# The first projections of a diffusion trunk: column sums, transposes and products in another order on TensorE, with two instead of three chunks of adaLN products on VectorE

## The chip, the cores and the metric

The kernel runs on one core of one Trainium2 chip. The metric is the device time of one execution in microseconds (us), median of several runs. Engines are named as in the profile: PE is TensorE (matmuls; PEld its weight loads), DVE is VectorE, ACT is ScalarE, POOL is GpSimd, SP is SyncE, whose queue starts nearly all DMAs. Matmuls write to PSUM; the kernel holds eight tiles (banks) of 128 x 512 floats there, six under the name `acc` and two under the name `aux`.

## The reference, cut to what matters

The whole program is two layers of a diffusion backbone over 256 latent tokens `x` and 256 context tokens `ctx`, width 1024. Only the head of layer 0 is touched:

```python
sh_m, sc_m, g_m, sh_f, sc_f, g_f = split(silu(c) @ ada_w[0] + ada_b[0], 6)   # adaLN, once for c, once for c_ctx
h = rms_norm(x, norm_mix[0]) * (1 + sc_m) + sh_m                            # and the same for ctx
y = h @ conv_w1 + b1                                                        # 1024 -> 2048
a, g = split(y, 2);  y = a * sigmoid(g)                                     # then a depthwise convolution
```

So before the first product `h @ conv_w1` can be made for a chunk of 128 features, the scale and the shift of that chunk must be there, and they are themselves products of `silu(c)` with 1 MB of `ada_w` per chunk (128 shift columns and 128 scale columns).

## The kernel before, in words

The 1024 features are eight chunks f = 0 to 7 of 128. The start of the program (L394 to L461) goes through them once and makes, for each:

- the loads (`start_load`, L363): 1 MB of adaLN weights and 256 KB of `conv_w1` for the first two output pairs, all on SP's queue;
- the adaLN sums. For most chunks (those not in `ADA_ROWS`) TensorE makes them: `ada_sums` (L239, eight matmuls of 256 columns, called S(f) below) into one PSUM bank, ACT copies the bank out (L245), two narrow matmuls sum its four partial rows into columns (`ada_cols`, L251, called C(f)), and ACT adds the bias (`ada_mods`, L258). For the chunks in `ADA_ROWS` DVE makes them instead: `start_rows` (L382), four products of 128 x 1024 with an accumulated sum, and a small bias add (L389);
- `mod_scale` on DVE (L270, writes `modA`);
- four transposes of the normed tokens into one PSUM bank (L437, called T(f)), scale and shift on ACT in that bank (L450, two halves), and the split of the result into a rounded part `ah_h` (L324, DVE) and the rest `al_h` (L325, DVE);
- the same split of the weights: `wh_w1a` on ACT (L163) and `wl_w1a` on DVE (L171);
- twelve products (L200 to L202): for two output pairs (`a0`,`g0` and `a1`,`g1`, four `acc` banks held through all eight chunks) three matmuls each, the second of which needs `al_h` and the third `wl_w1a`.

Everything of this is pinned: `pin` is `tc.keep_in_program_order`, so the order of the program text is the order on every engine's queue. An engine runs its queue in order. Before the change a chunk's round in the loop is T(f), C(f) and the modulation, then the products of chunk f-1, with S(f+1) between them; S and T both take their bank from `aux`, which has two. `ADA_ROWS` is (3, 5, 7), and `ROWS_AT` says how many of the DVE products stand ahead of the scale on ACT and how many behind the split in each round.

Ahead of that loop, `cond` is spread over the partitions by 16 matmuls (`crow`, L134) through the `aux` banks, each evicted by ACT (L136). Behind it, ACT takes the first weight block of the next pair (`wh_w1b`, L163), loads a function table, takes the sigmoid of `g0` (L467) and the biased `a0` (L479), POOL multiplies them (L480), and DVE's convolution taps (L538, L540) start on that. TensorE goes on at once with the products of the third pair (`g<-wh_w1b`).

Of the kernel before, what the change touches and what calls it, by code (L numbers as in the profile page):

```python
# [11 lines left out]
AF = mybir.ActivationFunctionType  # L12
# [3 lines left out]
P = 128  # L16
D = 1024
KC = D // P
TOK = 256
# [22 lines left out]
ADA_PAIRS += [(16 + 2 * i, 17 + 2 * i) for i in range(4)]  # L42
ADA_PAIRS += [(24 + f, 32 + f) for f in range(8)]

ADA_ROWS = (3, 5, 7)
ADA_PE = [i for i in range(20) if i not in ADA_ROWS]
ROWS_AT = [(0, 0), (0, 2), (1, 1), (1, 1), (1, 1), (1, 1), (1, 1), (0, 0)]
K_PAIRS = 2
GROUPS = [4, 4, 4, 4, 4, 4, 4, 4]
POOL = [6, 6, 6, 6, 6, 6, 6, 5]  # L50
# [31 lines left out]
def trunk_kernel(ctx: ExitStack, tc, x_in, ctx_in, cond, small, consts, rope, dist, ada, adas, adat,  # L82
                 w1a, w1b, dwd, w2, gu0, dn0, dn0l, wqk, wv, wg, wo, gu1, dn1, out):
    nc = tc.nc
# [10 lines left out]
    def acc(name):  # L95
        return ps.tile([P, 512], F32, tag="acc", name=name, bufs=6)

    def aux(name):
        return ps.tile([P, 512], F32, tag="aux", name=name, bufs=2)


    one = cp.tile([P, 1], F32, name="one")
# [9 lines left out]
    ident = cst[:, 0:128]  # L112
# [15 lines left out]

    crow0 = cv.tile([P, 4, 2 * YW], F32, tag="z4", name="crow0", bufs=Z4)
    crow0 = crow0.rearrange("p q t -> p (q t)")[:, 0:2 * D]  # L130
    for q in range(4):
        pc = aux("crow")
        for j in range(4):
            tc.keep_in_program_order(nc.tensor.matmul(pc[32 * j:32 * j + 32, :], one[0:1, :].to_broadcast([1, 32]),  # L134
                                 junk0[0:1, 512 * q:512 * q + 512], start=True, stop=True))
        nc.scalar.activation(crow0[:, 512 * q:512 * q + 512], pc, AF.Silu)  # L136

    load_tokens(x_in, 0)

# [9 lines left out]
    pin = tc.keep_in_program_order  # L149
# [6 lines left out]
    def split_hi(raw, n, name, also=lambda i: None):  # L156

        out_ = []
        for c in range(0, n, 1024):
            m = min(1024, n - c)  # L160
            hi = wp.tile([P, 1024], F32R, tag="wh", name="wh_" + name, bufs=WSPLIT)
            lo = wp.tile([P, 1024], F32R, tag="wl", name="wl_" + name, bufs=WSPLIT)
            also(nc.scalar.activation(hi[:, :m], raw[:, c:c + m], AF.Copy))  # L163
            out_.append((hi, lo))
        return out_

    def split_lo(raw, n, parts, eng=None, also=lambda i: None):
# [190 lines left out]
    h = new_act(pA, "h0")  # L358
# [3 lines left out]
    w1r, w1br, ada0 = {}, {}, {}  # L362

    def start_load(i):
        if i in ADA_ROWS:
            ada0[i] = [sp.tile([P, D], F32, tag="k4", name=f"raw_ada{i}", bufs=K4) for _ in range(2)]
            for c in range(2):
                pin(nc.sync.dma_start(ada0[i][c], adas[ADA_ROWS.index(i), :, D * c:D * c + D]))
        else:
# [22 lines left out]
    xs = normed([0, 1], xn4[:, 0:2, :]) + normed([2, 3], xn4[:, 2:4, :])  # L392
# [2 lines left out]
    dw = smc("dw").rearrange("p (c t) -> p c t", c=KC)  # L395
    dwb = smc("dwb")
    cn = smc("cn")
    pa0 = [(acc(f"a{p}"), acc(f"g{p}")) for p in range(K_PAIRS)]
    w1a_w = {}

    def start_products(f, p):
        wh, wl = w1a_w[f]
        for g in range(2):
            c = slice(256 * p + 128 * g, 256 * p + 128 * g + 128)
            mm3(pa0[p][g], (wh[:, c], wl[:, c]), (h[0][:, f, :], h[1][:, f, :]), f == 0, f == KC - 1, pin)

    def start_sums(f):
        if f < KC and f not in ADA_ROWS:
            pa = ada_sums(f, ada0.pop(f), aux, pin)
            ada_mid0[f] = pa, ada_rows(f, pa, pin)  # L410

    def start_w(f):
        if f < KC:
            w1a_w[f] = split_hi(w1r[f], 256 * K_PAIRS, f"w1a{f}", pin)[0]
            split_lo(w1r[f], 256 * K_PAIRS, [w1a_w[f]], None, pin)

    ada_mid0 = {}
    for n in range(3):
        start_load(n)
    start_sums(0)  # L420
    gens = {f: start_rows(f) for f in ADA_ROWS}
    rows = [f for f in ADA_ROWS for _ in range(4)]

    def piece(n):
        for _ in range(min(n, len(rows))):
            next(gens[rows.pop(0)])

    for f in range(KC + 1):
        if f + 3 < KC:
            start_load(f + 3)  # L430
        elif f + 3 == KC:
            w1_load(K_PAIRS)
            w1_load(K_PAIRS + 1)
        if f < KC:
            pt = aux("tr_start")
            for i in range(4):
                pin(nc.tensor.transpose(pt[:, P * i:P * i + P], xs[i][:, P * f:P * f + P], ident))  # L437
            if f == 1:
                start_products(0, 0)
            if f not in ADA_ROWS:  # L440
                ada_cols(f, *ada_mid0[f], pin)
                ada_mods(f, ada_mid0[f][0], pin)
            else:
                for _ in gens[f]:
                    pass
            pin(mod_scale(0, 0, f, f + 1))
            piece(ROWS_AT[f][0])
            for s in range(2):
                A, B = mod_AB(0, 0, f, s)
                pin(nc.scalar.activation(pt[:, TOK * s:TOK * s + TOK], pt[:, TOK * s:TOK * s + TOK], AF.Identity,  # L450
                                         scale=A, bias=B))
            if f == 0:
                start_w(0)
            split_to(h[0][:, f, :], h[1][:, f, :], pt, pin)
            piece(ROWS_AT[f][1])
        if f > 1:
            start_products(f - 1, 0)
        start_sums(f + 1)
        start_w(f + 1)
        if f:  # L460
            start_products(f - 1, 1)  # L461

    yc = cv.tile([P, KC, 512], F32, tag="big", name="yc")

# [168 lines left out]
    for step in range(KC):  # L633
        d = step - 1
        c = max(step - 2, 0) if step > 1 else None
        if d >= 0:
            pool_taps(d)
        if step < K_PAIRS:
            pa, pg = pa0[step]
            sg = sgs[step] or glu_gate(step, pg)  # L640
        else:
            if step == 3:
                pg, pa = acc(f"g{step}"), acc(f"a{step}")
            else:
                pa, pg = acc(f"a{step}"), acc(f"g{step}")
# [44 lines left out]
        if step >= KC - 3:  # L690
            i = 2 * (step - KC + 3)
# [8 lines left out]
    c, d = KC - 2, KC - 1  # L700
# [89 lines left out]
    nh, pt = ptk[:, 8:12], ptk[:, 12:16]  # L790
# [45 lines left out]
    crow = ad.tile([P, 2, D], F32, name="crow")  # L836
# [26 lines left out]
    for n in range(2):  # L863
# [7 lines left out]
        for t, k in order:  # L871
# [11 lines left out]
            if n and (t, k) == (1, KC - 1):  # L883
                mod_scale(0, 1)
                h = new_act(pB, "h0f")
# [24 lines left out]
    for gi, (j0, gn) in enumerate(groups):  # L910
        hid = new_act(pA, f"hid{gi}")
        for j in range(j0, j0 + gn):
# [3 lines left out]
            pa, pb = acc(f"fa{j}"), acc(f"fb{j}")  # L916
# [33 lines left out]
        else:  # L950
            for n in range(2):
# [4 lines left out]
                for t, k in order:  # L956
# [5 lines left out]
                    if n and (t, k) == (1, gn - 1):  # L962
# [3 lines left out]
                        h = new_act(pB, "h1")  # L966
# [100 lines left out]
    for hd in range(HEADS):  # L1067
# [41 lines left out]
        for which in range(2):  # L1109
            pt = aux(f"qkT{hd}{which}").rearrange("p (d t) -> p d t", d=2)  # L1110
# [94 lines left out]
        else:  # L1205
# [11 lines left out]
            h = new_act(pB, "h1f")  # L1217
# [233 lines left out]
```

## Time and profile before

| | us |
|---|---|
| median of 3 runs | 1101.7 (1098.86 to 1102.46) |
| the profiled execution | 1103.33 |
| its span in the trace | 1101.2 |
| PE busy in the span | 1069.0 (97%) |
| DVE, ACT, POOL busy | 700.6, 417.5, 161.6 |

The profiled execution's own time is 2.1 us more than its span, and 1.6 us over the median of the runs. The share of busy PE is high over the whole span, so a table by stretches is needed to see what bounds the first 60 us. [...]

### The profile page before, as it was taken

What the parts mean: (1) busy time and instruction counts of PE and PEld (TensorE: products, weight loads), DVE (VectorE), ACT (ScalarE), POOL (GpSimd) and SP (SyncE); (2) the same over time, 40 slices, a digit from 0 to 9 for tenths busy, and PEclk for the clock granted to TensorE, in tenths of its full rate; (3) what the DMA queues carried; (4) which work ended last, traced back from release to release, by engine and by line L of the source; (5) the groups of instructions that cost most, each with busy time, mean ns of one, the idle gap of its engine ahead of it and who ended that gap; (6) DMA issues with size and microseconds to landing.
All of it is one profiled execution on the core that took longest, in us unless ns stands there. A gap on an engine that the chain in (4) does not pass through costs nothing.

```text
span 1101.2 us, 13492 instructions
## 1 busy us (share of the span) xinstructions
PE 1069.0 (97%) x5302; PEld 845.0 (77%) x5302; DVE 700.6 (64%) x1147; ACT 417.5 (38%) x607; POOL 161.6 (15%) x119
## 2 busy tenths in 40 slices
PE   6989998999999999999999999999999989999998
PEld 2766654789888888888888788888888868888886
DVE  3988873757999877545644796366364555555445
ACT  4474463343222122212232564234333454444442
POOL 0077853030000000000000330000000461000000
PEclk8999998999999999999999999999999999999999
DMA  9469778732566576533313342334333344455551
GB/s 372 181 179 264 223 195 348 265 115 99 191 248 249 201 296 234 186 114 116 115 59 132 135 143 106 115 134 155 113 115 115 115 152 155 172 190 191 190 182 49
DMA packets 35185, 190.29 MB, mean 173 GB/s; under 512 B 3953, under 2 KB 4401, under 8 KB 16177
## 3 DMA queue, kind: packets, MB, share of 16 engines
q1 hardware_dynamic: 34688, 187.87, 49.0%
q10 hardware_dynamic: 434, 1.55, 0.4%
q8 instruction: 42, 0.69, 0.3%
q14 instruction: 21, 0.17, 0.0%
HBM read 185.99 MB, written 3.42 MB: 172 GB/s over the span
## 4 chain that ended last, share of the span: by engine, by line
PE 86%; DVE 6%; DMA 4%; ACT 3%; issue 1%; SPq 0%; POOL 0%; ACTq 0%; DVEq 0%
PE u L202 4%; PE fa L201 4%; PE u L200 4%; PE u L201 4%; PE fa L202 4%; PE fb L201 4%; PE fb L202 4%; PE fa L200 4%; PE fb L200 4%; PE v L201 3%; PE v L202 3%; PE v L200 3%; PE dn L201 3%; PE dn L202 3%; PE dn L200 3%; PE cv L507 2%
## 5 line engine op out<-in xcount | busy, mean ns | idle before, releaser
L171 DVE TENSOR_TENSOR wl_gu<-raw_gu,wh_gu 128x1024 fp32r<-128x1024 f32 x76 | 92.2, 1223 | 82.6 <-ACT wh_gu L163 81.7
L163 ACT ACTIVATE wh_gu<-raw_gu 128x1024 fp32r<-128x1024 f32 x84 | 88.0, 1058 | 139.6 <-PE fb L201 52.6
L851 DVE SCALAR_TENSOR_TENSOR junk<-raw_adat,crow 128x1024 f32<-128x1024 f32 x80 | 97.5, 1219 | 0.9
L171 DVE TENSOR_TENSOR wl_dn<-raw_dn,wh_dn 128x1024 fp32r<-128x1024 f32 x38 | 46.5, 1224 | 45.3 <-ACT wh_dn L163 45.0
L200 PE MATMUL fa<-ah_h0f,wh_gu 128*128 128x512 f32 (+1 forms) x192 | 72.0, 376 | 1.0 <-DVE ah_h0f L324 1.0
L201 PE MATMUL fa<-al_h0f,wh_gu 128*128 128x512 f32 (+1 forms) x192 | 72.3, 376 | 0.1
L200 PE MATMUL fb<-ah_h0f,wh_gu 128*128 128x512 f32 (+1 forms) x192 | 72.1, 376 | 0.0
L202 PE MATMUL fa<-ah_h0f,wl_gu 128*128 128x512 f32 (+1 forms) x192 | 72.0, 375 | 0.0
L202 PE MATMUL fb<-ah_h0f,wl_gu 128*128 128x512 f32 (+1 forms) x192 | 72.0, 375 | 0.0
L201 PE MATMUL fb<-al_h0f,wh_gu 128*128 128x512 f32 (+1 forms) x192 | 72.0, 375 | 0.0
L163 ACT ACTIVATE wh_dn<-raw_dn 128x1024 fp32r<-128x1024 f32 x38 | 40.3, 1060 | 80.1 <-PE dn L202 35.5
L200 PE MATMUL u<-wh_gu,ah_h1f 128*128 128x512 f32 x160 | 63.5, 397 | 0.0
L171 POOL TENSOR_TENSOR wl_qk<-raw_qk,wh_qk 128x1024 fp32r<-128x1024 f32 x4 | 9.6, 2401 | 362.8 <-DVE res L355 350.3
L202 PE MATMUL u<-wh_gu,al_h1f 128*128 128x512 f32 x160 | 62.8, 393 | 0.0
L201 PE MATMUL u<-wl_gu,ah_h1f 128*128 128x512 f32 x160 | 62.2, 390 | 0.0
L523 POOL TENSOR_TENSOR pacc<-pacc,pr 128x512 f32<-128x512 f32 x39 | 58.8, 1508 | 17.8 <-ACT pr L522 15.5
L540 DVE SCALAR_TENSOR_TENSOR lacc<-y,sm,lacc 128x512 f32<-128x512 f32 x65 | 49.1, 755 | 2.1
L201 PE MATMUL v<-wl_v,ah_h 128*128 128x512 f32 x128 | 50.4, 393 | 0.0
L202 PE MATMUL v<-wh_v,al_h 128*128 128x512 f32 x128 | 50.1, 391 | 0.0
L200 PE MATMUL dn<-wh_dn,ah_hid 128*128 128x512 f32 x128 | 49.9, 390 | 0.0
L201 PE MATMUL dn<-wl_dn,ah_hid 128*128 128x512 f32 x128 | 49.8, 389 | 0.0
L202 PE MATMUL dn<-wh_dn,al_hid 128*128 128x512 f32 x128 | 49.8, 389 | 0.0
(308 smaller groups left out, 2669.5 us busy)
## 6 DMA issues: line engine op xcount, KB each, us to landing
raw_gu<-in_gu_dram SPq DMA_DIRECT2D x44, 1024.0 KB, 4.8
raw_adat<-in_adat_dram SPq DMA_DIRECT2D x28, 1024.0 KB, 4.9
raw_dn<-in_dn_dram SPq DMA_DIRECT2D x19, 1024.0 KB, 4.8
raw_ada<-in_ada_dram SPq DMA_DIRECT2D x10, 1024.0 KB, 10.8
z<-yd SPq DMA_DIRECT2D x32, 284.5 KB, 4.9
raw_qk<-in_wqk_dram SPq DMA_DIRECT2D x8, 1024.0 KB, 4.7
raw_v<-in_wv_dram SPq DMA_DIRECT2D x8, 1024.0 KB, 4.8
raw_g<-in_wg_dram SPq DMA_DIRECT2D x8, 1024.0 KB, 4.8
```

The lines of the kernel that those rows point to most:

```text
L163: also(nc.scalar.activation(hi[:, :m], raw[:, c:c + m], AF.Copy))
L171: also((eng or nc.vector).tensor_tensor(lo[:, :m], raw[:, c:c + m], hi[:, :m].bitcast(F32), op=ALU.subtract))
L200: also(nc.tensor.matmul(o, a[0], b[0], start=first, stop=False))
L201: also(nc.tensor.matmul(o, a[0], b[1], start=False, stop=False))
L202: also(nc.tensor.matmul(o, a[1], b[0], start=False, stop=last))
L507: pin(nc.tensor.matmul(cb[32 * q:32 * q + 32, :], dg[:, g, q, :], m, start=(g == 0), stop=(g == n - 1)))
L523: pin(nc.gpsimd.tensor_tensor(pacc, pacc, pr, op=ALU.add))
L540: pin(nc.vector.scalar_tensor_tensor(cacc, a, w, cacc, op0=ALU.mult, op1=ALU.add))
L851: pin(nc.vector.scalar_tensor_tensor(junk, raw[:, c, :], 1.0, crow[:, s, :], op0=ALU.mult, op1=ALU.mult, accum_out=mods[l][:, c0 + c, s:s ...
```

## The change

Four things change, all in the first 60 us.

1. The `crow` matmuls write four `acc` banks, not two `aux` banks in turn; ACT's evictions move in the text, and the banks `a0`, `g0`, `a1`, `g1` are taken afterwards.
2. S(f) takes its bank from `acc` (two are left there), so `aux` holds nothing but transposes.
3. The loop is written as a pipeline: in round f stand T(f+1), then the first three products of chunk f, then C(f+1) and the whole modulation of chunk f+1 (ACT and DVE), then the other nine products of chunk f, then S(f+2). The weight split of a chunk stands behind the split of its tokens.
4. `ADA_ROWS` is (4, 6), not (3, 5, 7), so TensorE makes the sums of one chunk more and DVE four products less; `ROWS_AT` puts the DVE products into rounds 2 to 5, between the rounds' tokens.

```diff
-ADA_ROWS = (3, 5, 7)
+ADA_ROWS = (4, 6)
-ROWS_AT = [(0, 0), (0, 2), (1, 1), (1, 1), (1, 1), (1, 1), (1, 1), (0, 0)]
+ROWS_AT = [(0, 0), (0, 0), (0, 3), (1, 0), (0, 3), (1, 0), (0, 0), (0, 0)]
...
+    pcs = [acc(f"crow{q}") for q in range(4)]
     for q in range(4):
-        pc = aux("crow")
...
-            pa = ada_sums(f, ada0.pop(f), aux, pin)
+            pa = ada_sums(f, ada0.pop(f), acc, pin)
...
-        if f < KC:
-            pt = aux("tr_start")
-            for i in range(4):
-                pin(nc.tensor.transpose(pt[:, P * i:P * i + P], xs[i][:, P * f:P * f + P], ident))
-            if f == 1:
-                start_products(0, 0)
-            if f not in ADA_ROWS:
-                ada_cols(f, *ada_mid0[f], pin)
-                ada_mods(f, ada_mid0[f][0], pin)
-            else:
-                for _ in gens[f]:
-                    pass
-            pin(mod_scale(0, 0, f, f + 1))
-            piece(ROWS_AT[f][0])
...
-            split_to(h[0][:, f, :], h[1][:, f, :], pt, pin)
-            piece(ROWS_AT[f][1])
-        if f > 1:
-            start_products(f - 1, 0)
-        start_sums(f + 1)
-        start_w(f + 1)
-        if f:
-            start_products(f - 1, 1)
+        piece(ROWS_AT[f][0])
+        more = f + 1 < KC
+        if more:
+            start_T(f + 1)
+        start_products(f, 0, 0)
+        if more:
+            start_cols(f + 1)
+            start_h(f + 1)
+        start_products(f, 0, 1)
+        start_products(f, 1, 0)
+        start_products(f, 1, 1)
+        start_sums(f + 2)
+        piece(ROWS_AT[f][1])
```

`start_T`, `start_cols` and `start_h` are the old loop's lines as functions; `start_h` ends with the weight split `start_w(f)`.

On DVE, from the low part of chunk 3's weights (`wl_w1a_316` before, `wl_w1a_344` now) to the tokens of the row chunk behind it. Before, `raw_ada_287` and `raw_ada_288` are the row weights of chunk 5:

```order
L171 TENSOR_TENSOR wl_w1a_316<-raw_w1a_205,wh_w1a_315 128x512
L389 TENSOR_TENSOR mods_111<-mods_111,sm 128x2x2
L270 SCALAR_TENSOR_TENSOR modA_113<-mods_111,sm 128x2
L382 SCALAR_TENSOR_TENSOR junk_77,mods_111<-raw_ada_287,crow_84 128x1024
L324 CAST ah_h_121<-tr_start 128x512
L325 TENSOR_TENSOR al_h_122<-tr_start,ah_h_121 128x512
L382 SCALAR_TENSOR_TENSOR junk_77,mods_111<-raw_ada_287,crow_84 128x1024
L171 TENSOR_TENSOR wl_w1a_360<-raw_w1a_242,wh_w1a_359 128x512
```

Now, `raw_ada_275` and `raw_ada_276` are the row weights of chunk 4, and `wl_w1a_381` is chunk 4's:

```order
L170 TENSOR_TENSOR wl_w1a_344<-raw_w1a_232,wh_w1a_343 128x512
L381 SCALAR_TENSOR_TENSOR junk_77,mods_107<-raw_ada_275,crow_84 128x1024 x2
L381 SCALAR_TENSOR_TENSOR junk_77,mods_107<-raw_ada_276,crow_84 128x1024 x2
L388 TENSOR_TENSOR mods_107<-mods_107,sm 128x2x2
L269 SCALAR_TENSOR_TENSOR modA_109<-mods_107,sm 128x2
L323 CAST ah_h_117<-tr_start 128x512
L324 TENSOR_TENSOR al_h_118<-tr_start,ah_h_117 128x512
L170 TENSOR_TENSOR wl_w1a_381<-raw_w1a_279,wh_w1a_380 128x512
```

The products that stood singly, ahead of a cast and behind a split, now stand four in a row between the weights of chunk 3 and the scale of chunk 4; the same stands between chunks 5 and 6.

On PE, where a chunk with sums on TensorE follows. Before, `ada_348` is chunk 4's sum bank and `w1a_315` are the weights of chunk 3:

```order
L437 MATMUL tr_start<-cst,xn_125 128x128 x4
L251 MATMUL ada_348<-cst,adasb 128x2 x2
L200 MATMUL a_174<-ah_h_121,wh_w1a_315 128x512
L201 MATMUL a_174<-al_h_122,wh_w1a_315 128x512
L202 MATMUL a_174<-ah_h_121,wl_w1a_316 128x512
L200 MATMUL g_175<-ah_h_121,wh_w1a_315 128x512
```

Now, `ada_393` is chunk 5's sum bank and `w1a_380` are the weights of chunk 4:

```order
L238 MATMUL ada_393<-raw_ada_322,csil 32x256 x8
L418 MATMUL tr_start<-cst,xn_121 128x128 x4
L199 MATMUL a_226<-ah_h_117,wh_w1a_380 128x512
L200 MATMUL a_226<-al_h_118,wh_w1a_380 128x512
L201 MATMUL a_226<-ah_h_117,wl_w1a_381 128x512
L250 MATMUL ada_393<-cst,adasb 128x2 x2
L199 MATMUL g_227<-ah_h_117,wh_w1a_380 128x512
```

The column sums of a chunk stood ahead of all products of the chunk before it; now they stand behind the first three of them.

## Rows read from the trace of the kernel before

**Rows 1.** The table by stretches, busy time of each engine in two stretches of 10 us, with granted clock and DMA.

```profile
core 0: us, PE busy (x) PEld busy (x) DVE busy (x) ACT busy (x) POOL busy (x), PEclk, DMA share, GB/s
20.00:30.00 10.00, 8.83 (x38) 6.34 (x39) 4.43 (x8) 2.39 (x6) 0.00 (x0) 0.52 1.04 414
...
40.00:50.00 10.00, 9.24 (x58) 6.74 (x56) 9.77 (x20) 4.58 (x12) 0.00 (x0) 1.00 0.09 34
```

**Rows 2.** The chain of waits that ended last, in order of time: start, length, what. A load of row weights, a pair of DVE products, and the end of the stage.

```profile
9.95 12.01 DMA raw_ada<-in_adas_dram
...
47.71 1.22 DVE junk L382 x2
...
55.42 1.92 ACT wh_w1b L163 x2
...
60.00 1.20 POOL y L480
```

**Rows 3.** Instructions in order of time (start, length, engine, line, what; in brackets the idle time before it and what ended it): chunk 0 and the way of chunk 1 from its column sums to its split.

```profile
12.53 1.93 PE L239 MATMUL ada<-raw_ada,csil 128*32 128x256 f32 x16 [0.56 <-DMA raw_ada<-in_ada_dram]
...
14.39 1.12 PE L437 MATMUL tr_start<-cst,xn 128*128 128x128 f32 x4
...
14.52 0.39 ACT L245 ACTIVATE adasb<-ada 128x256 f32<-128x256 f32 x1 [1.89 <-PE ada L239]
...
15.30 0.84 PE L251 MATMUL ada<-cst,adasb 128*128 128x2 f32 x4
...
16.64 1.07 PE L239 MATMUL ada<-raw_ada,csil 128*32 128x256 f32 x16 [0.50 <-ACT mods L258]
...
20.67 1.08 PE L437 MATMUL tr_start<-cst,xn 128*128 128x128 f32 x4 [2.96 <-DVE al_h L325]
...
24.11 0.85 PE L251 MATMUL ada<-cst,adasb 128*128 128x2 f32 x4
25.00 0.41 ACT L258 ACTIVATE mods<-ada,sm 128x2 f32<-128x2 f32 x2 [5.73 <-PE ada L251]
...
25.64 1.11 ACT L450 ACTIVATE tr_start<-tr_start,mods,modA 128x256 f32<-128x256 f32 x2 [0.23 <-DVE modA L270]
...
26.78 0.69 DVE L324 CAST ah_h<-tr_start 128x512 fp32r<-128x512 f32 x1 [1.18 <-ACT tr_start L450]
...
27.51 0.69 DVE L325 TENSOR_TENSOR al_h<-tr_start,ah_h 128x512 fp32r<-128x512 f32 x1
...
28.11 1.21 DVE L382 SCALAR_TENSOR_TENSOR junk<-raw_ada,crow 128x1024 f32<-128x1024 f32 x1
...
30.52 0.69 DVE L171 TENSOR_TENSOR wl_w1a<-raw_w1a,wh_w1a 128x512 fp32r<-128x512 f32 x1
```

**Rows 4.** The same view later: a weight split, the bias of a row chunk and its scale on ACT; the splits of chunks 3 and 7; the first product of the third pair on PE.

```profile
35.11 0.69 DVE L171 TENSOR_TENSOR wl_w1a<-raw_w1a,wh_w1a 128x512 fp32r<-128x512 f32 x1
...
35.71 0.15 DVE L389 TENSOR_TENSOR mods<-mods,sm 128x4 f32<-128x4 f32 x1
...
36.16 1.11 ACT L450 ACTIVATE tr_start<-tr_start,mods,modA 128x256 f32<-128x256 f32 x2 [3.01 <-DVE modA L270]
...
38.03 0.69 DVE L325 TENSOR_TENSOR al_h<-tr_start,ah_h 128x512 fp32r<-128x512 f32 x1
...
56.18 0.69 DVE L325 TENSOR_TENSOR al_h<-tr_start,ah_h 128x512 fp32r<-128x512 f32 x1
...
59.55 0.39 PE L200 MATMUL g<-ah_h,wh_w1b 128*128 128x512 f32 x1
```

**Rows 5.** The same view, PE alone, for its pace: two products at the lower clock, then column sums and transposes with what follows each, and ten products in a row at the higher clock.

```profile
21.98 0.63 PE L201 MATMUL a<-al_h,wh_w1a 128*128 128x512 f32 x1
...
22.41 0.63 PE L202 MATMUL a<-ah_h,wl_w1a 128*128 128x512 f32 x1
...
30.31 0.51 PE L251 MATMUL ada<-cst,adasb 128*128 128x2 f32 x4
...
30.68 0.48 PE L200 MATMUL a<-ah_h,wh_w1a 128*128 128x512 f32 x1
...
33.53 0.60 PE L437 MATMUL tr_start<-cst,xn 128*128 128x128 f32 x4
...
33.88 0.47 PE L200 MATMUL a<-ah_h,wh_w1a 128*128 128x512 f32 x1
...
40.24 0.39 PE L202 MATMUL a<-ah_h,wl_w1a 128*128 128x512 f32 x1
...
42.28 0.39 PE L202 MATMUL g<-ah_h,wl_w1a 128*128 128x512 f32 x1
```

**Rows 6.** PE in short stretches late in the program (busy time, granted clock, DMA): an idle gap and the clock behind it.

```profile
904.00:905.00 1.00, 0.00 (x0) 1.00 0.97 410
...
908.00:909.00 1.00, 1.00 (x4) 0.50 0.97 401
...
911.00:912.00 1.00, 1.00 (x6) 1.00 0.83 303
```

**Rows 7.** Instructions of PE that waited, 69 to 92 us.

```profile
71.94 3.64 PE L507 MATMUL cv<-z,dg 128*32 128x512 f32 x32 [1.35 <-issue]
...
82.58 3.64 PE L507 MATMUL cv<-z,dg 128*32 128x512 f32 x32 [1.32 <-ACT pr L522]
```

More of the change, by code (lines that the diff above doesn't have):

```diff
@@ L130, in trunk_kernel @@
     crow0 = crow0.rearrange("p q t -> p (q t)")[:, 0:2 * D]
+    pcs = [acc(f"crow{q}") for q in range(4)]
     for q in range(4):
-        pc = aux("crow")
         for j in range(4):
-            tc.keep_in_program_order(nc.tensor.matmul(pc[32 * j:32 * j + 32, :], one[0:1, :].to_broadcast([1, 32]),
+            tc.keep_in_program_order(nc.tensor.matmul(pcs[q][32 * j:32 * j + 32, :], one[0:1, :].to_broadcast([1, 32]),
                                  junk0[0:1, 512 * q:512 * q + 512], start=True, stop=True))
-        nc.scalar.activation(crow0[:, 512 * q:512 * q + 512], pc, AF.Silu)
     load_tokens(x_in, 0)
@@ L397, in trunk_kernel, with start_products, start_T, start_cols @@
     cn = smc("cn")
-    pa0 = [(acc(f"a{p}"), acc(f"g{p}")) for p in range(K_PAIRS)]
     w1a_w = {}
[L401 to L405, printed above, removed]
+    def start_products(f, p, g):
+        wh, wl = w1a_w.get(f)
+        c = slice(256 * p + 128 * g, 256 * p + 128 * g + 128)
+        mm3(pa0[p][g], (wh[:, c], wl[:, c]), (h[0][:, f, :], h[1][:, f, :]), f == 0, f == KC - 1, pin)
+    ada_mid0, tr0 = {}, {}
     def start_sums(f):
         if f < KC and f not in ADA_ROWS:
-            pa = ada_sums(f, ada0.pop(f), aux, pin)
+            pa = ada_sums(f, ada0.pop(f), acc, pin)
             ada_mid0[f] = pa, ada_rows(f, pa, pin)
     def start_w(f):
-        if f < KC:
-            w1a_w[f] = split_hi(w1r[f], 256 * K_PAIRS, f"w1a{f}", pin)[0]
-            split_lo(w1r[f], 256 * K_PAIRS, [w1a_w[f]], None, pin)
-    ada_mid0 = {}
+        w1a_w[f] = split_hi(w1r[f], 256 * K_PAIRS, f"w1a{f}", pin)[0]
+        split_lo(w1r[f], 256 * K_PAIRS, [w1a_w[f]], None, pin)
+    def start_T(f):
+        tr0[f] = aux("tr_start")
+        for i in range(4):
+            pin(nc.tensor.transpose(tr0[f][:, P * i:P * i + P], xs[i][:, P * f:P * f + P], ident))
+    def start_cols(f):
+        if f not in ADA_ROWS:
+            ada_cols(f, *ada_mid0[f], pin)
+            ada_mods(f, ada_mid0[f][0], pin)
+        else:
+            for _ in gens[f]:
+                pass
+    def start_h(f):
+        pt = tr0.pop(f)
+        pin(mod_scale(0, 0, f, f + 1))
+        for s in range(2):
+            A, B = mod_AB(0, 0, f, s)
+            pin(nc.scalar.activation(pt[:, TOK * s:TOK * s + TOK], pt[:, TOK * s:TOK * s + TOK], AF.Identity,
+                                     scale=A, bias=B))
+        split_to(h[0][:, f, :], h[1][:, f, :], pt, pin)
+        start_w(f)
     for n in range(3):
@@ L426, in piece @@
             next(gens[rows.pop(0)])
-    for f in range(KC + 1):
+    start_cols(0)
+    start_T(0)
+    start_h(0)
+    for q in range(4):
+        nc.scalar.activation(crow0[:, 512 * q:512 * q + 512], pcs[q], AF.Silu)
+    start_sums(1)
+    pa0 = [(acc(f"a{p}"), acc(f"g{p}")) for p in range(K_PAIRS)]
+    for f in range(KC):
         if f + 3 < KC:
@@ L433, in trunk_kernel @@
             w1_load(K_PAIRS + 1)
-        if f < KC:
-            pt = aux("tr_start")
-            for i in range(4):
-                pin(nc.tensor.transpose(pt[:, P * i:P * i + P], xs[i][:, P * f:P * f + P], ident))
-            if f == 1:
-                start_products(0, 0)
-            if f not in ADA_ROWS:
-                ada_cols(f, *ada_mid0[f], pin)
-                ada_mods(f, ada_mid0[f][0], pin)
-            else:
-                for _ in gens[f]:
-                    pass
-            pin(mod_scale(0, 0, f, f + 1))
-            piece(ROWS_AT[f][0])
[L448 to L453, printed above, removed]
-            split_to(h[0][:, f, :], h[1][:, f, :], pt, pin)
-            piece(ROWS_AT[f][1])
-        if f > 1:
-            start_products(f - 1, 0)
-        start_sums(f + 1)
-        start_w(f + 1)
-        if f:
-            start_products(f - 1, 1)
+        piece(ROWS_AT[f][0])
[11 more added lines that the diff above has]
+        piece(ROWS_AT[f][1])
     yc = cv.tile([P, KC, 512], F32, tag="big", name="yc")
```

## The prediction, made before the changed kernel ran

> **What bounds the kernel now.** I read the table by stretches first, since a share of 97% for PE over the whole span says nothing of one stage. [...] Then the chain of waits, in order of time: up to 22 us it hangs on the load of chunk 3's row weights, afterwards on DVE (pairs of products, splits) with a scale on ACT in each round, and after 55.42 us on ACT and POOL, up to the first convolution input `y` at 60.00 us [rows 2]. The instructions in order of time say what the early stretch waits for: T(1) starts at 20.67 us after 2.96 us of idle PE, because its bank in `aux` is chunk 0's until `al_h` has been written [rows 3]. Chunk 3's split starts at 38.03 us and chunk 7's at 56.18, so two chunks take 9.08 us there [rows 4].
>
> So the stage has two halves: up to chunk 2 waits and a slow clock, then DVE. The sums below give c(f), the time at which the column sums of chunk f end on PE; all else of a chunk hangs on it.
>
> **The change, part by part.** *From column sums to split.* In the rows of chunk 1, C ends at 24.96, the scale starts on ACT at 25.64 (0.68 later), the cast at 26.78, `al_h` at 27.51 (2.55 after c), and the next DVE instruction at 28.11, 3.15 after c [rows 3]. Now that next one is the weight split of 0.69, so it ends 3.84 after c. Behind it PE has the third product of the chunk (0.23: ten products lie 0.227 apart, 40.24 to 42.28) and C of the next chunk (0.37: 30.31 to 30.68) [rows 5]. With 0.05 for the handover, as between C's end and ACT's start (24.96 to 25.00) [rows 3], a chunk takes 3.84 + 0.05 + 0.23 + 0.37 = 4.5 us. PE's own work is 12 x 0.227 + 0.35 (T) [rows 5] + 1.07 (S) [rows 3] + 0.37 = 4.5, so at the higher clock both just match.
>
> *The first chunks.* S(0) waits for its load at 12.53 us as before, and ACT's copy ends at 14.91 [rows 3]. C(0) now stands ahead of T(0): 14.96 + 0.84 = 15.80, T(0) then takes 1.12 and ends at 16.92, and the scale waits for T(0) where it waited for C(0): start at 16.96, as if c(0) were 16.3. Before it was 16.14, so this swap gains nothing. Then c(1) = 20.8 against 24.96, c(2) = 25.3, c(3) = 29.8. T(1) and S(1) need no bank of chunk 0 any more, and that is where the gain comes from. Chunk 3's `al_h` starts at 29.8 + 2.55 = 32.35 against 38.03 [rows 4]: 5.7 us gained.
>
> *The two row chunks.* Four DVE products stand in one piece behind `wl_w1a` of chunk 3, ahead of the scale of chunk 4, and again between 5 and 6. Nothing on DVE can pass them, and C(5) on PE stands behind the products of chunk 4, which need chunk 4's split. Step by step from c(3): `wl_w1a` starts at +3.15, the next instruction 0.60 later (35.11 to 35.71) [rows 4]; two products take 2.41 (28.11 to 30.52) [rows 3], four 4.82, to +8.57; from the bias to the scale on ACT 0.45 (35.71 to 36.16) [rows 4], +9.02; cast 1.14 later, `al_h` 0.73 after that (26.78 to 27.51) [rows 3], `wl_w1a` 0.60 after that, ended at +12.18; handover, product and C(5) 0.65: c(5) = c(3) + 12.8 = 42.6, and c(7) = 55.4. Two chunks took 9.08 before, so 3.7 are lost in each of two rounds, 7.4 in all, against a gain of 5.7. Three row chunks of DVE work have become two, but the products that lay beside ACT's scale (DVE was never idle there) now lie with nothing beside them, and DVE is idle for the scale.
>
> *The end of the stage.* ACT ends chunk 7's scale 1.8 after c(7), at 57.2, then has this chunk's weight split (0.6, estimated: DVE's takes 0.69 on the same tile, ACT's `wh_w1b` blocks of twice the width 0.96 each [rows 2]) that stood earlier before, so it comes to `wh_w1b` at 57.8 against 55.42 [rows 2]. What follows on ACT is unchanged, so `y` comes 2.4 us later. PE's way: 24 products of chunks 6 and 7 at 0.227 and the wait for `wl_w1a` (59.2) give 59.2 + 0.05 + 12 x 0.227 = 62.0 against 59.55 [rows 4], also 2.4.
>
> *The clock.* PE now idles in each row round: it ends T(5) at c(3) + 2.04 + 0.35, waits for `wl_w1a` (33.64), then 0.28 + 2.04 + 1.07 + 0.35 = 37.4, and chunk 4's cast ends at 40.65, a gap of 3.3 us, twice. Before, the gap of 2.96 us ahead of T(1) was followed by the stretch at 0.52 [rows 1, 3], and a gap around 904 us by some 3 us at 0.50 [rows 6]. So I take the lower level behind both gaps. There a product takes 0.43 (21.98 to 22.41) [rows 5] and C 0.85 [rows 3], so the last step before c(5) and c(7) is longer by 0.20 + 0.48 = 0.68 each: 1.4 in all. Bounds: nothing (the gaps are forgiven) and 2.6, if the twelve products of chunk 7 run at that level too (12 x 0.20 on PE, of which the 1.35 us of idle PE before the first convolution [rows 7] hide half).
>
> *The rest.* The `crow` matmuls lose two waits on ACT but S(0) waits for its load anyway. S of one chunk more (1.07) lies in PE's row-round idle time. The row weights: chunk 3's landed at 21.96 [rows 2]; a chunk's 1.25 MB at 414 GB/s [rows 1] is 3.2 us, so chunk 4's are there at about 25 (estimate), 8 us ahead of need. SP's queue: S(0) must free a raw buffer before chunk 3's load can be issued, at 14.5 instead of 9.6, while the loads of chunks 1 and 2 still fill the DMA; cost nothing, and if the DMA ran dry meanwhile, at most the 4.9 us of delay less the 5 that chunk 3's S has in hand (its data at 22, its turn at 25.3 + 2.04 = 27.3): nothing again.
>
> Sum: 2.4 + 1.4 = 3.8 us, own range 2.4 to 5. Behind the stage the DVE taps start from `y`, so I pass it on whole. The profiled execution would go from 1103.3 to 1107.1; it stood 1.6 over the median of the runs, so against that median: 1101.7 + 3.8 = 1105.5.
>
> **The rivals.** *The slow clock stays in the first half too.* For it: PE between 17 and 20 us has only sums, transposes and three single products, and it fell to 0.50 there before. Against: there is no gap of 3 us left. One spell as long as that of 904 us costs half of its 3.3 us, 1.6; the stretch up to 29.6, at 12 x 0.43 + 1.93 + 0.91 (T to C, 14.39 to 15.30) + 0.85 = 8.8 us per chunk [rows 3, 5], costs 0.7 for chunk 1 and 4.3 for chunk 2. 1107 to 1110.5, about 1108.5. [...]
>
> *The convolution stage swallows it: not slower.* PE idles 1.35 and 1.32 us before the first two convolution groups [rows 7]. If those waits are for something that does not move with `y`, PE takes 2.7 of the 3.8 us back, from 71.94 us on: 1101.7 + 1.1 = 1102.8, or 1101.4 with the clock kept. Against: what is waited for there comes out of `y` by the bounce through memory and ACT's taps.
>
> *The row products cost nothing: faster.* If DVE reached chunk 5 as fast as before, the 5.7 us would stay: 1101.7 - 5.7 = 1096. For it: DVE has four products of 1.21 us less to do [rows 3]. Against: the order on its queue, and C(5) behind chunk 4's products. It wins if the step from the split of chunk 3 to that of chunk 5 stays below 11.9 us (9.08 + half of 5.7).
>
> **How the numbers follow.** The forecast has 50%, the slow first half 22%, the swallowed delay 16%, the kept gain 10%, anything else 2%. About 0.3% (3.3 us) is what a measurement can tell from no change: of the forecast's range 2.4 to 5, some 36 of the 50 lie above it. Slower: 0.36 + 0.21 = 0.57; same: 0.14 + 0.16 + 0.02 = 0.32; faster 0.11. The range goes from 1101 (the swallowed delay) to 1109.5 (most of the slow first half), and leaves out the kept gain and the rest of the slow clock.
>
> **What would show it.** Right: `al_h` of chunks 1, 2 and 3 near 23.4, 27.9 and 32.4 us; four row products without a break on DVE at about 33.5; a gap of some 3 us on PE that ends with a product that waited for the cast; `al_h` of chunk 7 near 58 to 59; `y` on POOL at 62 to 64. Wrong: chunk 3's split later than 35 us (then the clock or a load), chunk 5's less than 11.9 us after chunk 3's (then the row round is not what I take it for), or `y` later by 3 us and the end not.

## The result and the profile after

The changed kernel takes 1105.85 us (median of 11 runs, 1102.0 to 1108.55) beside 1100.88 us (11 runs, 1098.04 to 1102.8) for the kernel before: ratio 1.0041 [1.0026, 1.0055], slower by 4.5 us (1100.88 x 0.0041) to 5.0 (the medians). The profiled execution took 1106.84 us, its span 1105.0 against 1101.2. The busy times over the whole span show nothing of the loss: PE is busy for 1072.4 us, 97% as before.

The table by stretches shows the stage, and answers to [rows 1] (PEclk is the granted clock of TensorE as a share of its full one):

```profile
core 0: us, PE busy (x) PEld busy (x) DVE busy (x) ACT busy (x) POOL busy (x), PEclk, DMA share, GB/s
20.00:30.00 10.00, 10.00 (x72) 7.24 (x72) 4.26 (x8) 4.83 (x12) 0.00 (x0) 1.00 1.02 405
30.00:40.00 10.00, 8.73 (x52) 5.83 (x51) 7.16 (x14) 2.04 (x5) 0.00 (x0) 1.00 0.76 289
40.00:50.00 10.00, 7.75 (x24) 5.97 (x25) 5.48 (x11) 3.92 (x9) 0.00 (x0) 0.66 0.24 100
50.00:60.00 10.00, 7.15 (x42) 4.70 (x41) 6.11 (x12) 3.35 (x9) 0.00 (x0) 0.94 0.00 1
```

From 20 to 30 us PE is now full, and at the higher clock from about 21 us on (the durations tell this, C(1) 0.77 us at 20.62 and C(2) 0.50 at 25.68, not the column PEclk, which reads 1.00 also from 16 to 18 us, where S(1) takes 1.94 us). From 40 us on nothing is full: DVE, which was busy for 9.77 of 10 us there, is busy for 5.48 and PE for 7.75 at a granted clock of 0.66. A stage in which each engine waits for another has taken the place of one that DVE bounded.

The instructions in order of time (start, length; the idle time before it in brackets), which answer to [rows 3] and [rows 4]. First the pipeline's pace, then the row round of chunk 4, then the end of the stage:

```profile
20.62 0.77 PE L250 MATMUL ada<-cst,adasb 128*128 128x2 f32 x4
...
25.68 0.50 PE L250 MATMUL ada<-cst,adasb 128*128 128x2 f32 x4
...
30.51 0.50 PE L250 MATMUL ada<-cst,adasb 128*128 128x2 f32 x4
...
33.55 0.69 DVE L324 TENSOR_TENSOR al_h<-tr_start,ah_h 128x512 fp32r<-128x512 f32 x1
...
34.76 1.22 DVE L381 SCALAR_TENSOR_TENSOR junk<-raw_ada,crow 128x1024 f32<-128x1024 f32 x1
...
38.55 1.22 DVE L381 SCALAR_TENSOR_TENSOR junk<-raw_ada,crow 128x1024 f32<-128x1024 f32 x1
...
39.82 0.17 DVE L388 TENSOR_TENSOR mods<-mods,sm 128x4 f32<-128x4 f32 x1
...
42.25 0.76 PE L199 MATMUL a<-ah_h,wh_w1a 128*128 128x512 f32 x1 [3.20 <-ACT adasb L244]
...
44.08 0.85 PE L250 MATMUL ada<-cst,adasb 128*128 128x2 f32 x4
...
45.41 0.16 DVE L269 SCALAR_TENSOR_TENSOR modA<-mods,sm 128x2 f32<-128x2 f32 x1 [1.98 <-ACT mods L257]
...
47.48 0.69 DVE L324 TENSOR_TENSOR al_h<-tr_start,ah_h 128x512 fp32r<-128x512 f32 x1
...
57.75 0.50 PE L250 MATMUL ada<-cst,adasb 128*128 128x2 f32 x4
...
60.79 0.69 DVE L324 TENSOR_TENSOR al_h<-tr_start,ah_h 128x512 fp32r<-128x512 f32 x1
...
65.13 1.19 POOL L493 TENSOR_TENSOR y<-y,sg 128x512 f32<-128x512 f32 x1 [63.76 <-ACT y L492]
...
77.00 3.64 PE L520 MATMUL cv<-z,dg 128*32 128x512 f32 x32 [1.39 <-issue]
```

And chunk 5's split in the kernel before:

```profile
47.10 0.69 DVE L325 TENSOR_TENSOR al_h<-tr_start,ah_h 128x512 fp32r<-128x512 f32 x1
```

Chunk 3's split starts 4.5 us earlier than before (33.55 against 38.03 [rows 4]). Then four products of DVE stand in a row, 34.76 to the bias add at 39.82, while PE idles for 3.20 us and comes back at about half the pace: the granted clock is 0.50 from 42 to 48 us, and the column sums at 44.08 take 0.85, not 0.50. DVE waits in turn: `modA` of chunk 5 comes after 1.98 us of idle DVE, because PE made C(5) only behind chunk 4's first three products. Chunk 5's split is 0.4 us late (47.48 against 47.10), chunk 7's is 4.6 us late (60.79 against 56.18), `y` 5.1 (65.13 against 60.00 [rows 2]), the first convolution group 5.1 (77.00 against 71.94 [rows 7]).

PE alone in a full round of the pipeline, behind the column sums at 25.68, which answers to [rows 5]; between 26.37 and 27.99 stand six more products:

```profile
26.04 0.49 PE L199 MATMUL g<-ah_h,wh_w1a 128*128 128x512 f32 x1
26.37 0.40 PE L200 MATMUL g<-al_h,wh_w1a 128*128 128x512 f32 x1
...
27.99 0.40 PE L201 MATMUL g<-ah_h,wl_w1a 128*128 128x512 f32 x1
28.32 1.07 PE L238 MATMUL ada<-raw_ada,csil 128*32 128x256 f32 x16
29.32 0.66 PE L418 MATMUL tr_start<-cst,xn 128*128 128x128 f32 x4
29.73 0.48 PE L199 MATMUL a<-ah_h,wh_w1a 128*128 128x512 f32 x1
30.05 0.39 PE L200 MATMUL a<-al_h,wh_w1a 128*128 128x512 f32 x1
```

The next instruction begins before the one ahead of it has ended, so the pace is read from start to start: 0.36 us behind the column sums, then nine products up to 28.32, the sums 1.00, the transposes 0.41, three products to 30.51.

The chain of waits (start, length, what) hangs in the row round on the products, then on ACT, PE and ACT again, where before it went from DVE to ACT's scale and back in each round [rows 2]:

```profile
38.55 1.24 DVE junk L381 x2
...
42.25 0.76 PE a L199
...
44.28 0.66 PE ada L250 x4
...
60.58 1.89 ACT wh_w1b L162 x2
```

### The profile page after: what moved, and what is told of

Same layout as the page of the kernel before. It is cut to its first block, busy times and chain, and to the rows that moved or that the text cites. A ratio compares the mean times of both kernels' runs of the same rounds, so it can differ in the third digit from the quotient of the medians.

```text
span 1105.0 us, 13526 instructions
## 1 busy us (share of the span) xinstructions
PE 1072.4 (97%) x5322; PEld 847.0 (77%) x5322; DVE 696.3 (63%) x1138; ACT 418.2 (38%) x610; POOL 161.6 (15%) x119
## 4 chain that ended last, share of the span: by engine, by line
PE 85%; DVE 4%; DMA 4%; ACT 3%; POOL 2%; issue 2%; SPq 0%; ACTq 0%; POOLq 0%
PE fa L200 4%; PE fa L201 4%; PE fb L201 4%; PE fa L199 4%; PE fb L200 4%; PE fb L199 4%; PE u L201 3%; PE u L199 3%; PE u L200 3%; PE v L200 3%; PE v L201 3%; PE v L199 3%; PE dn L199 3%; PE dn L200 3%; PE dn L201 3%; PE g L199 2%
```

## The experiments

Eleven runs were made, eight of other kernels and three of the two kernels as they are. Ratios are against the kernel before, timed on the same chip with each set (1101.52 us for the first four, 1101.19 for the next four; 1101.31 in a single run beside the last three). `y` is the start of its product on POOL: 60.00 before, 65.13 after. The first part of the change, the banks of `crow`, was not run alone; S(0), which stands behind it, starts at 12.33 to 12.53 us in three traces of the kernel before and at 12.23 and 12.48 in two of the changed one, so no effect of it can be seen.

**1. One product less in each block.**

```diff
-ROWS_AT = [(0, 0), (0, 0), (0, 3), (1, 0), (0, 3), (1, 0), (0, 0), (0, 0)]
+ROWS_AT = [(0, 0), (0, 1), (0, 3), (0, 1), (0, 3), (0, 0), (0, 0), (0, 0)]
```

> The changed kernel with one of each row chunk's four DVE products moved one round ahead, behind the weight split of the chunk before, where DVE waits for the next scale. Theory (the DVE products that stand in one piece are the loss): each product taken out of a block brings its 1.26 us, the moved one lies in idle time; y on POOL from 65.1 to about 62.7 us, time about 2.4 us below the changed kernel's, 1103.4. Rival (the loss is PE's: a pace of 4.8 us per chunk and the clock behind the gaps): no change, y at 65.

Measured: 1103.24 us, ratio 1.0016 [1.0005, 1.0027], `y` at 62.53, as the theory has it. Each product that stands beside another wait takes 1.3 us off a round (2.6 in two). The gaps of PE shrink to 1.93 and 0.97 us; the first is still followed by the lower clock (0.50 from 42 to 47 us), the second not (1.00 from 50 to 60):

```profile
40.92 0.63 PE L199 MATMUL a<-ah_h,wh_w1a 128*128 128x512 f32 x1 [1.93 <-ACT adasb L244]
...
53.57 0.47 PE L199 MATMUL a<-ah_h,wh_w1a 128*128 128x512 f32 x1 [0.97 <-ACT adasb L244]
```

**2. The same eight products, each where DVE waits anyway:** one behind `modA`, while ACT scales, and one at the end of a round.

```diff
-ROWS_AT = [(0, 0), (0, 0), (0, 3), (1, 0), (0, 3), (1, 0), (0, 0), (0, 0)]
+ROWS_AT = [(0, 0), (0, 1), (0, 1), (0, 1), (0, 1), (0, 0), (0, 0), (0, 0)]
+ROWS_IN = [0, 0, 1, 1, 1, 1, 0, 0]
...
         pin(mod_scale(0, 0, f, f + 1))
+        piece(ROWS_IN[f])
```

> The changed kernel with the eight DVE products spread singly: one behind modA (beside ACT's scale) and one behind the weight split in chunks 2 to 5. Theory: the row rounds go at PE's pace of 4.8 us per chunk like the others, chunk 7's column sums end at about 50.5 instead of 58.3, no gap of 3 us on PE and no fall of the clock there; y at about 57.5, time about 1098, below the kernel before. Rival: PE's pace and the first half bound it, y above 62 and time above 1103.

Measured: 1098.02 us, ratio 0.9970 [0.9958, 0.9982], `y` at 56.64: 8.5 us earlier than in the changed kernel, with the same work. In the order of time a product fills the time between `modA` and the cast, and no gap of PE over 0.5 us is left between 20 and 58 us:

```profile
31.20 0.16 DVE L270 SCALAR_TENSOR_TENSOR modA<-mods,sm 128x2 f32<-128x2 f32 x1 [0.32 <-ACT mods L258]
31.28 1.22 DVE L382 SCALAR_TENSOR_TENSOR junk<-raw_ada,crow 128x1024 f32<-128x1024 f32 x1
32.43 0.08 DVE L382 DVE_READ_ACCUMULATOR junk<-raw_ada,crow 128x1 f32 x1
32.54 0.69 DVE L324 CAST ah_h<-tr_start 128x512 fp32r<-128x512 f32 x1
```

**3. No row products:** `ADA_ROWS = ()`, so TensorE makes the sums of all eight chunks; nothing is left out.

> The changed kernel with all eight chunks' sums on TensorE and no DVE products (ADA_ROWS empty). It takes S(4), C(4), S(6), C(6) more on PE, 2 x 1.4 us. Theory: all rounds take 4.8 us, chunk 7's column sums end at 21.4 + 6 x 4.8 = 50.2, y at about 57, time about 1097.5. Rival (TensorE's sums are the dearer ones, or the raw buffers' loads come late): y at 60 or later, time 1101 or more.

Measured: 1097.52 us, ratio 0.9966 [0.9954, 0.9978], `y` at 56.81. The column sums start every 4.8 us (30.18, 34.96, 39.79, 44.61, 49.42) with PE full: the pipeline runs at PE's pace throughout, and ends no earlier than with the eight products well placed.

**4. The kernel before with the sums' bank alone,** in the old order and with the old rows:

```diff
-            pa = ada_sums(f, ada0.pop(f), aux, pin)
+            pa = ada_sums(f, ada0.pop(f), acc, pin)
```

> The kernel before with one edit: S(f) takes its bank from acc, so T(1) does not wait for chunk 0's split. Theory (the early gain comes from the banks, not from the pipeline's order): T(1) at about 18 instead of 20.7, chunk 1's column sums end at about 22 instead of 25, chunk 3's al_h 2 to 3 us earlier than 38.0; then DVE's pace of 9.1 us for two chunks as before, so y at 57 to 58 and time about 1098.5. Rival (the early gain needs the pipeline's order): y at 59.5 to 60, time as before.

Measured: 1097.27 us, ratio 0.9961 [0.9947, 0.9975], `y` at 56.69. This one line gains 4.3 us (2.8 to 5.8 by the interval), though the loads, which the chain of waits names for the first 22 us [rows 2], are as they were. T(1) no longer waits for chunk 0's `al_h` (16.59 against 20.67 [rows 3]), PE stays at the higher pace behind it (C(1) takes 0.50 us, where it took 0.85 [rows 3]), and the 3.3 us that chunk 3 is ahead (34.72 against 38.03) stay to the end of the stage. PE idles for 2.21 and 1.60 us on the way, and the granted clock stays at 1.00 behind both (the products behind them take 0.39 to 0.40 us):

```profile
16.59 0.66 PE L437 MATMUL tr_start<-cst,xn 128*128 128x128 f32 x4
...
19.46 0.47 PE L200 MATMUL a<-ah_h,wh_w1a 128*128 128x512 f32 x1 [2.21 <-DVE ah_h L324]
...
21.33 0.50 PE L251 MATMUL ada<-cst,adasb 128*128 128x2 f32 x4
...
30.07 0.50 PE L200 MATMUL a<-ah_h,wh_w1a 128*128 128x512 f32 x1 [1.60 <-DVE ah_h L324]
...
34.72 0.69 DVE L325 TENSOR_TENSOR al_h<-tr_start,ah_h 128x512 fp32r<-128x512 f32 x1
...
52.87 0.69 DVE L325 TENSOR_TENSOR al_h<-tr_start,ah_h 128x512 fp32r<-128x512 f32 x1
```

**5. The changed kernel with its gaps of PE filled** by twelve extra products whose result is not used:

```diff
             start_T(f + 1)
+        if f in ADA_ROWS:
+            pf = acc("fill")
+            for _ in range(12):
+                pin(nc.tensor.matmul(pf, w1a_w[f - 1][0][:, 0:128], h[0][:, f - 1, :], start=True, stop=True))
```

> The changed kernel with twelve products more on TensorE in each of the two gaps (2.7 us, into a free bank, their result unused), ahead of the first product of chunks 4 and 6. Theory (the half-rate spells cost about 0.9 us at chunk 5 and up to 1 at the end): the clock stays at 1.00 from 41 to 64 us, chunk 5's column sums end near 44.0 instead of 44.9, y at about 64, time 1 to 2 us below the changed kernel's, 1104 to 1105. Rival (the clock costs nothing, since DVE is waited for): y at 65, time 1106.

Measured: 1103.15 us, ratio 1.0016 [1.0007, 1.0025], `y` at 64.12. The granted clock is 1.00 behind both gaps and up to `y`, and the order's own price is left over:

```profile
20.47 0.50 PE L250 MATMUL ada<-cst,adasb 128*128 128x2 f32 x4
...
33.14 0.69 DVE L324 TENSOR_TENSOR al_h<-tr_start,ah_h 128x512 fp32r<-128x512 f32 x1
...
38.40 3.02 PE L469 MATMUL fill<-ah_h,wh_w1a 128*128 128x512 f32 x12
...
41.84 0.47 PE L199 MATMUL a<-ah_h,wh_w1a 128*128 128x512 f32 x1 [0.43 <-ACT adasb L244]
...
46.46 0.69 DVE L324 TENSOR_TENSOR al_h<-tr_start,ah_h 128x512 fp32r<-128x512 f32 x1
...
59.77 0.69 DVE L324 TENSOR_TENSOR al_h<-tr_start,ah_h 128x512 fp32r<-128x512 f32 x1
```

The step from chunk 3's split to chunk 5's is 13.32 us, where the changed kernel takes 13.93: the slow clock costs 0.61 in the first round. From chunk 5 to chunk 7 it is 13.31 in both, so nothing in the second. The other 0.4 us in `y` were there before the first gap (33.14 against 33.55): PE came up earlier in this execution, C(1) took 0.50 us and not 0.77, and chunk 1's split starts at 23.51 against 23.94. The median fell by 2.7, more than `y`, but each ratio is uncertain by 0.1% to 0.15%, and what the run has beyond 0.6 to 1.0 us is not explained.

**6. C(5) and C(7) ahead of the row chunk's products:**

```diff
             start_T(f + 1)
+        if f in ADA_ROWS:
+            start_cols(f + 1)
         start_products(f, 0, 0)
         if more:
-            start_cols(f + 1)
+            if f not in ADA_ROWS:
+                start_cols(f + 1)
```

> The changed kernel with the column sums C(5) and C(7) ahead of the first three products of chunks 4 and 6 on TensorE, nothing else moved. Theory (DVE waits for C(5) behind those products, 45.41 less 43.43 = 2.0 us): DVE goes from chunk 4's weight split to chunk 5's modA at once, 1.3 to 2.0 us per row round; y at 61.5 to 62.5, time about 1102.5 to 1103. Rival (the four DVE products are all of the loss): y at 64.5 to 65, time 1105 to 1106.

Measured: 1102.53 us, ratio 1.0010 [1.0000, 1.0020], `y` at 62.12, 3 us earlier than in the changed kernel, as the theory has it. C(5) now starts with chunk 4's split and no longer behind three products that need it. What it still waits for is ACT's copy of its bank (L244), which stands on ACT behind chunk 4's scale and weight split, so the four DVE products ahead of that scale still hold it up:

```profile
41.94 0.37 ACT L244 ACTIVATE adasb<-ada 128x256 f32<-128x256 f32 x1
...
42.36 1.01 PE L250 MATMUL ada<-cst,adasb 128*128 128x2 f32 x4 [3.18 <-ACT adasb L244]
...
54.62 0.61 PE L250 MATMUL ada<-cst,adasb 128*128 128x2 f32 x4 [1.15 <-ACT adasb L244]
```

**7. The changed order with the sums back in `aux`:**

```diff
-            pa = ada_sums(f, ada0.pop(f), acc, pin)
+            pa = ada_sums(f, ada0.pop(f), aux, pin)
```

> The changed kernel with S(f) back in aux, the new order kept. Theory (the order alone frees most of the early waits, since T(1) stands behind S(1) and waits only for chunk 0's split at 19.2): T(1) at 19.3 instead of 18.4, everything behind it 0.9 us later, y at about 66, time about 1107. Rival (the early gain is the banks' alone): chunk 3's al_h back at 37 to 38 instead of 33.6, y at 69 or later, time 1109 or more.

Measured: 1111.06 us, ratio 1.0080 [1.0067, 1.0093], `y` at 70.63: the theory fell, and the rival's times hold (its `al_h` of chunk 3, 37 to 38, came at 36.83). I had forgotten a wait: in the row rounds the next chunk's transposes need the bank that the row chunk holds until its split, so PE waits 4.5 us for it, twice.

```profile
46.25 0.63 PE L418 MATMUL tr_start<-cst,xn 128*128 128x128 f32 x4 [4.49 <-DVE al_h L324]
...
60.73 1.09 PE L418 MATMUL tr_start<-cst,xn 128*128 128x128 f32 x4 [4.48 <-DVE al_h L324]
```

**8. Experiment 4 with two row chunks:**

```diff
-ADA_ROWS = (3, 5, 7)
-ROWS_AT = [(0, 0), (0, 2), (1, 1), (1, 1), (1, 1), (1, 1), (1, 1), (0, 0)]
+ADA_ROWS = (3, 6)
+ROWS_AT = [(0, 0), (0, 2), (1, 1), (0, 1), (1, 1), (1, 0), (0, 0), (0, 0)]
...
-            pa = ada_sums(f, ada0.pop(f), aux, pin)
+            pa = ada_sums(f, ada0.pop(f), acc, pin)
```

> The kernel before with S(f) in acc as in the fourth run, and two row chunks (3 and 6) instead of three, their products still single, beside ACT's scale and behind the split. Theory (DVE's products set the old order's pace of 9.1 us for two chunks, PE's would be 4.8 for a chunk with sums and 3.4 without): y at 55 to 56 against 56.7 with three, time 1096 to 1097, the fastest so far. Rival (PE's 4.8 us already bounds it): y at 56.7 or later, time 1097.5.

Measured: 1097.98 us, ratio 0.9973 [0.9961, 0.9986], `y` at 57.87: the theory missed, and a row chunk less on DVE gains nothing that can be told over experiment 4 (1097.27). The rival's numbers hold. From chunk 3's split to chunk 7's it takes 17.89 us, where experiment 4 takes 18.15; in the rounds of chunks 4 and 5, at 4.94 and 4.86 us each, DVE waits 0.45 and 0.37 us for the bias behind the column sums, as the rival's pace would have it. The 1.2 us by which `y` is later than in experiment 4 were lost ahead of chunk 1's split (25.81 against 24.38), up to which the two kernels have the same text: PE came up later in this execution (C(1) at 22.65 against 21.33). So `y` of a single trace can be off by more than a microsecond, and 1.7 of the 3.1 us by which chunk 1 is ahead in experiment 4 come with the bank even when PE comes up late (before: 27.51). PE idles for 1.61 us ahead of chunk 2's first product, as in experiment 4, but here the granted clock is 0.56 from 33 to 34 us and 0.50 from 34 to 36:

```profile
31.50 0.51 PE L200 MATMUL a<-ah_h,wh_w1a 128*128 128x512 f32 x1 [1.61 <-DVE ah_h L324]
```

**9 to 11. Both kernels again, unchanged,** one execution each, because the mean granted clock differed between executions of the kernel before.

> The kernel before, unchanged, to see a second execution of it in full. Theory: the stretch at half rate from 19.4 to 29.6 us that the forecast took from the trace belongs to the one execution profiled, not to the kernel: that one had a mean granted clock of 0.991, while 51 other runs of it had a median of 0.996 to 0.997, some 9 us less at half rate. Then this trace shows PE at 1.00 from 20 to 30 us, al_h of chunk 3 at 36.5 to 37.5 us (38.03 in the first trace) and y on POOL at 58.5 to 59.5 (60.00). Rival: the early stretch is always there and the later ones (166 to 190 and 907 us) are what comes and goes: 0.5 to 0.6 from 20 to 30 us again, al_h of chunk 3 at 38, y at 60.

> The changed kernel, unchanged, to see a second execution of it in full. Its eleven runs had a mean granted clock of 0.989 to 0.996, median 0.991. Theory: the two stretches at half rate behind its gaps of PE (about 42 to 48 us and 59 to 62 us) are in every execution: 0.60 to 0.70 from 40 to 50 us again, y on POOL at 65.0 to 65.3. Rival: they come and go as in the kernel before: 1.00 from 40 to 50 us, y at 64.1 as with the extra products.

> The kernel before a third time, for the same question as the second. Theory: 1.00 from 20 to 30 us in most executions, al_h of chunk 3 at 36.5 to 37.5 us and y on POOL at 58.5 to 59.5. Rival: 0.5 to 0.6 there each time, al_h of chunk 3 at 38 and y at 60.

Measured: before again, 1100.72 us, `al_h` of chunk 3 at 37.68, `y` at 59.65; a third time, 1104.05 us, 37.94 and 59.91. After again, 1104.43 us, `y` at 65.22 and 0.66 from 40 to 50 us as in the first trace, so the theory for the changed kernel holds. The theory fell for the kernel before, in a way worth seeing. The second trace has 1.00 in the column of the granted clock from 20 to 30 us, where the first and third have 0.52:

```profile
20.00:30.00 10.00, 9.01 (x44) 6.64 (x44) 4.43 (x8) 2.39 (x6) 0.00 (x0) 1.00 1.03 412
```

And yet its instructions there are as slow as in [rows 3]:

```profile
16.46 1.94 PE L239 MATMUL ada<-raw_ada,csil 128*32 128x256 f32 x16 [0.50 <-ACT mods L258]
...
23.93 0.85 PE L251 MATMUL ada<-cst,adasb 128*128 128x2 f32 x4
25.28 1.94 PE L239 MATMUL ada<-raw_ada,csil 128*32 128x256 f32 x16 [0.51 <-ACT mods L258]
```

S(1) took 1.94 us (1.07 in the first trace and the third), so PE had not come up yet at all, and what lies ahead of the first recorded change reads as 1.00. The slow stretch is in all three executions of the kernel before (products still take 0.60 to 0.62 us at 29.20, 28.17 and 29.08); mean clocks of whole runs (0.991, 0.996 and 0.990 here) can't be compared where that stretch lies at the start. With `y` within 0.35 us, the three spans are 1101.2, 1098.6 and 1101.9: such scatter arises later, and `y` tells more of this stage than the end of one execution.

## Why the prediction was right

Right in sign and cause, and in size within its range: 1105.5 forecast, 1105.85 measured, at the upper end of the forecast's own range of 2.4 to 5 us later (4.5 to 5.0). That the two times lie 0.35 us apart is partly luck: the medians differ by 5.0 us where 3.8 was forecast, and the kernel before came out 0.8 us below the 1101.7 to which the 3.8 were added. `y` at 65.1 lies beyond the 62 to 64 that were named for it. By its own steps:

- **The first chunks.** The cause holds, a bank that no longer waits: experiment 4 shows it alone, worth 4.3 us. The size was too large: `al_h` of chunk 3 at 33.55, not 32.35, so 4.5 us gained and not 5.7. C(1) ended 0.6 later than forecast (21.39), and the pace is 4.8 us, not 4.5 (column sums at 25.68 and 30.51). Some 0.4 of the first 0.6 is the lower level, which lasted up to C(1) and which the forecast had only in a rival: in experiment 5, where PE came up earlier, C(1) ended at 20.97. The mis-sized term of the pace is PE's twelve products "x 0.227": in the full round of the trace after (25.68 to 30.51) they take 3.06 us and not 2.72, as three of them (behind C, behind T and ahead of S) are followed after 0.32 to 0.33 us, and the other terms came out at 0.36 (C), 1.00 (S) and 0.41 (T). PE sets this pace, not DVE's chain beside it.
- **The two row chunks.** The mechanism is as forecast: the four products stood in one piece, the scale behind them, C(5) behind chunk 4's products. Experiment 1 takes one product of the four out of each block (2.6 us of `y`), experiment 6 the three products from ahead of C(5) and C(7) (3.0), experiment 2 the blocks as a whole, and both waits go with them (8.5). Without the clock a round takes 13.3 us (experiment 5) where 12.8 was forecast: four products with their accumulator reads take 5.06 us, not 4.82, and the last product with C(5) 0.24 more than the 0.65 counted. Against 9.08 before that is 4.24 lost in each round, 8.5 in all, not 7.4.
- **The clock.** Both gaps of PE came (3.20 and 2.59 us, 3.3 forecast), with the lower level behind each (0.50 from 42 to 48 and from 59 to 62 us). But 0.61 us of it reached `al_h`, not 1.4: the second fall began between 58 and 59 us (0.87), when C(7) was done (57.75, 0.50).
- **The end of the stage.** At chunk 7's split the sum of the measured terms is -4.5 + 8.5 + 0.6 = 4.6, which is what the trace shows (60.79 against 56.18); the forecast had 3.1 there. From there to `y` it takes 4.34, not 3.82 (60.00 less 56.18): the 0.5 is the weight split on ACT, forecast at 0.6. So `y` is 5.1 late. The errors of the parts, +1.2, +1.1 and -0.8 us, cancelled only in part; the 1.5 left, less 0.1 on ACT, are the miss in `y` to rounding (65.13 against 63.8).
- **The rivals.** The slow clock did not stay in the first half: PE came up during C(1) at 20.62 us (it took 0.77, the next 0.50), and the ten microseconds behind it are full. The convolution stage swallows nothing: its first group still waits 1.39 us and starts 5.1 late. The row products are not free as placed (13.9 us from chunk 3 to chunk 5, where 11.9 was the limit); experiment 2 shows that elsewhere in this order they are, and experiment 3 that without them no more is to be had.

What brings PE up to the higher level is not shown. In the three traces of the kernel before, with the same instructions, it had come up by S(1) in the first and the third (1.07 us) and not in the second (1.94 us). The second also has the slow stretch of chunk 1 (C(1) 0.85 us, S(2) 1.94 us) with no fall ahead of it, so that stretch does not need the gap of 2.96 us that the forecast took for its cause.

So the change is two changes of opposite sign. The bank gains 4.3 us by itself (experiment 4). The new order needs that bank (experiment 7), gains nothing beyond it (2 and 3 are within the interval of 4), and with the row products in blocks gives back 8.4 us of `y` (65.13 against 56.69). The version to keep is the one of experiment 4, one line against the kernel before, faster than both: 1097.27 us. Experiments 2, 3 and 8 can't be told from it in time, with more lines changed.

## What to carry to other kernels

Look first for a buffer in which two unrelated things take turns: giving one of them a spare bank was worth more here (4.3 us) than a new order of the whole loop (nothing beyond it in experiments 2 and 3). Work for an engine that is not full belongs where this engine waits anyway; put in one piece ahead of an instruction that another engine needs, it is paid by both (here 4.24 us in each round for 5.06 us of products), and so is whatever stands behind it on a queue without needing it (C(5) and C(7): 3.0 us of `y`, experiment 6). In a pipeline count the handovers of the engine that becomes full, not only its work (here twelve products took 3.06 us, not 2.72).

## What the runs showed of the hardware

- Some handovers on TensorE take longer than others: a product behind column sums or transposes, or ahead of sums, is followed by the next instruction after 0.32 to 0.33 us (26.04 to 26.37, 29.73 to 30.05, 27.99 to 28.32 in the trace after), the other products of that round after 0.23. Why is not shown.
- The length of a gap of PE does not tell by itself whether the lower clock follows: 1.93 us in experiment 1 and 1.61 in experiment 8 were followed by it (products of 0.63 us, a granted clock of 0.50), 2.21 and 1.60 in experiment 4 were not (products of 0.39 to 0.40 us), nor 0.97 (1), 1.15 (6) and 0.43 (5), behind which the granted clock reads 1.00.
- In these traces the column of the granted clock reads 1.00 ahead of the first recorded change, at either level; only durations show it (kernel before, ahead of the fall at about 19.5 us: S(0) 1.93 us and S(1) 1.07, both beside 1.00; experiment 9: S(2) 1.94 us beside 1.00).
- Later in the program the clock falls or does not fall in executions of one kernel: the two traces of the changed kernel have 0.66 and 1.00 from 170 to 175 us, and their spans are 1105.0 and 1102.6 with `y` within 0.1 us.
